# Long convolution of a Hyena layer: the inverse transform computed for half the rows with the table stationary, against the full transform with the spectrum stationary

## The chip, the core and the metric

The kernel runs on one core of a Trainium2 chip. The core has five engines with a queue each: TensorE (PE, matrix products into PSUM), VectorE (DVE), ScalarE (ACT), GpSimd (POOL) and SyncE (SP, which issues the DMAs here). The metric is the device time of one execution in microseconds.

## The reference, cut to what matters

Four layers work on 256 context tokens and 256 latent tokens, 1024 features each. Layer 2 (of 0 to 3) mixes tokens with a Hyena block, and this is the only place that the change touches:

```python
def fft_longconv(u, k):
    L = u.shape[1]
    U = jnp.fft.rfft(u.astype(F32), n=2 * L, axis=1)
    K = jnp.fft.rfft(k, n=2 * L, axis=0)
    return jnp.fft.irfft(U * K[None], n=2 * L, axis=1)[:, :L].astype(u.dtype)

def hyena(h, w_in, b_in, w_short, b_short, ..., skip, w_out, b_out):
    u = dwconv(h @ w_in + b_in, w_short, b_short)
    x0, x1, v = jnp.split(u, 3, axis=-1)
    k = hyena_filter(L, ...)          # divided by the sum of its absolute values
    v = v * x1
    v = fft_longconv(v, k) + skip * v
    return (v * x0) @ w_out + b_out
```

It is run for the context and for the latent stream, so L is 256 and each transform has 512 points.

## The kernel before

Everything is fp32. A weight or an operand `a` of a product is split into a rounded part and the rest (`hi` and `lo`, type fp32r), and `mm3` (L157 to L160) makes a product of three matmuls: hi by hi, hi by lo, lo by hi. `load_w` (L144, L147) makes the two parts of each weight tile: ACT copies the rounded part, DVE subtracts. `split` (L169, L170) does the same for activations, again one ACT and one DVE instruction.

The layer holds its features on partitions: `V[o]`, o from 0 to 7, is the product v * x1 of 128 features, with 512 columns: 256 context tokens (stream s = 0), then 256 latent tokens (s = 1). The transforms are matrix products with tables. A unit of the transform, m from 0 to 7, is one stream (s = m mod 2) of the 256 features of the tiles o = 2 (m div 2) and o + 1.

- On the way in, the sequence is folded about its middle: `PQ` holds sums and differences of token n and token 255 - n, for n below 128. `flip_in(m)` (L1261) transposes these with four PE transposes, so that tokens lie on partitions, and splits them.
- `freq(m, f)` makes the frequencies of half f (f = 0 or 1) with 6 matmuls of 256 columns, multiplies them by the filter's spectrum (L1275 to L1279 on DVE, one copy on POOL, L1281) and splits the result `Y[m, f]` (L169 on ACT, L170 on DVE).
- `back(m, c)` (L1285) makes the tokens of tile o = 2 (m div 2) + c: four `mm3`, 12 matmuls. `Y` is stationary (128 frequencies by 128 features) and the table `inv` moves with 256 columns, one for each token. So the result has features on partitions, as V has. DVE then multiplies V by `skip` in place (L1294) and adds the result scaled by `rn` (L166, `g<-mm,rn,g`).

`conv()` is a generator that lays these pieces out in 21 steps, st = 0 to 20. In step st come, in this order, `flip_in(m)` if it is due (st = 2m + 1 for even m, st = 2m for odd m), `freq(st div 2 - 1, st mod 2)` if there is one, and from st = 5 on `back((st - 5) div 2, (st - 5) mod 2)`. One step is taken behind every input projection (`in_proj`: 24 matmuls of 512 columns). Twelve steps stand beside the projections of v and x1, eight beside those of x0. The last step stands alone, behind step 19 and ahead of the output projection. Behind each projection `short` runs a 3-tap convolution: two ACT instructions (L1241, L1242) and two on DVE (L166, `e<-e,par`). In the steps of x0, `gate(o)` multiplies V by x0 (L1329) and splits it (L169, L170) for the output projection, whose loop takes the tiles k = 0 to 7 in order.

The order of PE's instructions is the order of the code. That of DVE, ACT and POOL is chosen by a scheduler ahead of the run, and each of these engines then takes its instructions strictly in that order, waiting in front of any whose input is missing.

Of the kernel before, what the change touches and what calls it, by code (L numbers as in the profile page):

```python
# [15 lines left out]
AF = mybir.ActivationFunctionType  # L16
ALU = mybir.AluOpType
AX = mybir.AxisListType

P = 128  # L20
D = 1024
KT = D // P
T = 512
L = 256
# [32 lines left out]
def r(ap):  # L57
    return ap.bitcast(F32R)
# [25 lines left out]
def kernel(ctx: ExitStack, tc: tile.TileContext, xT, cT, cB, ada0, ada2, adaT1, adaT2, adaT3, prm, mlp, w_c, w_ug, w_o,  # L84
                         w_p1, w_p2, w_hi1, w_hi0, w_ho, w_fup, w_fd0, w_fd1, w_fd2, spec0, f_w3, decay, dft, c_dft, c_b, out,
                         layers=(0, 1, 2, 3), final=True):
    nc = tc.nc
# [8 lines left out]
    def ps_mm():  # L96
        return pm.tile([P, T], F32, tag="mm", name="mm")

    def ps_tr():
        return pm.tile([P, T], F32, tag="mm", name="tr")  # L100
# [4 lines left out]
    def e_tile(shape=None):  # L105
        return gp.tile(shape or [P, T], F32, tag="g", name="e")

    ident = const.tile([P, P], F32, name="ident")
# [12 lines left out]
    def col(name, *dims):  # L121
        o, n = COLS[name]
        return par[:, o:o + n]
# [31 lines left out]
    def mm3(ps, a, b, start, stop):  # L155
        ah, al = a
        bh, bl = b  # L157
        nc.tensor.matmul(out=ps, lhsT=r(ah), rhs=r(bh), start=start, stop=False)  # L158
        nc.tensor.matmul(out=ps, lhsT=r(ah), rhs=r(bl), start=False, stop=False)  # L159
        nc.tensor.matmul(out=ps, lhsT=r(al), rhs=r(bh), start=False, stop=stop)  # L160

    def both(t, f):
        return f(t[0]), f(t[1])

    def stt(o, a, s, b, op0, op1, **kw):
        nc.vector.scalar_tensor_tensor(out=o, in0=a, scalar=s, in1=b, op0=op0, op1=op1, **kw)  # L166
# [945 lines left out]
    rn = const.tile([P, KT], F32, name="rn")  # L1112
# [102 lines left out]
    def hyena(li, nm):  # L1215
# [10 lines left out]
        inv = both(di, lambda t: t.rearrange("p (k t) -> p k t", k=4))  # L1226
# [26 lines left out]
        V, VT, Y, PQ = [], {}, {}, {}  # L1253
        skip = col("hy_skip")

        def flip_in(m):
            jj, s = divmod(m, 2)
            tr = ps_tr()
            for t in range(2):
                for c in range(2):  # L1260
                    nc.tensor.transpose(out=tr[:, (2 * t + c) * P:(2 * t + c + 1) * P], in_=PQ[2 * jj + c][:, t, s, :], identity=ident)  # L1261
            VT[m] = (g_tile(), g_tile())
            split(VT[m][0], VT[m][1], tr)

        def freq(m, f):
            jj, s = divmod(m, 2)
            vt = VT[m]
            ps = ps_mm()
            for im in range(2):
                fc = 2 * im + f  # L1270
                mm3(ps[:, im * L:(im + 1) * L], both(fwd, lambda a: a[:, fc * P:(fc + 1) * P]),
                    both(vt, lambda a: a[:, im * L:(im + 1) * L]), True, True)
            t1, t2 = e_tile(), e_tile()
            kk = kfs[jj // 2][:, jj % 2, f]
            nc.vector.tensor_tensor(out=two(t1), in0=two(ps), in1=kk, op=ALU.mult)  # L1275
            nc.vector.tensor_tensor(out=t2[:, 0:L], in0=ps[:, 0:L], in1=kk[:, 1], op=ALU.mult)
            nc.vector.tensor_tensor(out=t2[:, L:T], in0=ps[:, L:T], in1=kk[:, 0], op=ALU.mult)
            nc.vector.tensor_tensor(out=t2[:, L:T], in0=t2[:, 0:L], in1=t2[:, L:T], op=ALU.subtract)
            nc.vector.tensor_tensor(out=t2[:, 0:L], in0=t1[:, 0:L], in1=t1[:, L:T], op=ALU.add)  # L1279
            if f == 0:  # L1280
                nc.gpsimd.tensor_copy(out=t2[0:1, :], in_=t1[0:1, :])  # L1281
            Y[m, f] = (g_tile(), g_tile())
            split(Y[m, f][0], Y[m, f][1], t2)

        def back(m, c):  # L1285
            jj, s = divmod(m, 2)
            o = 2 * jj + c
            ps = ps_mm()
            for f in range(2):
                for im in range(2):  # L1290
                    mm3(ps[:, 0:L], both(Y[m, f], lambda a: a[:, im * L + c * P:im * L + (c + 1) * P]),
                        both(inv, lambda a: a[:, 2 * im + f, :]), f == 0 and im == 0, f == 1 and im == 1)
            vo = V[o][:, s * L:(s + 1) * L]
            nc.vector.tensor_scalar(out=vo, in0=vo, scalar1=skip[:, o:o + 1], scalar2=None, op0=ALU.mult)  # L1294
            stt(vo, ps[:, 0:L], rn[:, o:o + 1], vo, ALU.mult, ALU.add)

        def conv():
            for st in range(21):
                m, i = divmod(st, 2)
                if m < 8 and i == 1 - m % 2:  # L1300
                    flip_in(m)
                if 0 <= m - 1 < 8:
                    freq(m - 1, i)
                if st >= 5:
                    back((st - 5) // 2, (st - 5) % 2)
                yield

        work = conv()
        for o in range(KT):
            if o >= 2:  # L1310
# [24 lines left out]
        for u in range(4):  # L1335
            w = load_pair(w_hi0[u], act=True)
            for c in range(2):
                o = 2 * u + c
# [221 lines left out]
```

## Time and profile before

| | us |
|---|---|
| median of 3 runs (2144.52 to 2145.59) | 2145.06 |
| the profiled execution, its own time | 2145.16 |
| its span | 2143.3 |
| PE busy in the span | 2096.1 (98%) |
| DVE busy | 1557.3 (73%) |
| ACT busy | 1287.5 (60%) |
| POOL busy | 236.2 (11%) |

The time of the execution is 1.86 us above the span of its instructions. Matmuls overlap: a busy PE says that some matmul was in flight, and what a matmul costs is read from the distance between the starts of two. DVE and ACT instructions also overlap a little at their ends. A matmul named `mm<-a,b` streams `a` and holds `b`. The Hyena layer's transforms lie between 1240 us and 1377 us of the span. TensorE's granted clock there is 1.00, the upper of its two levels (2.4 GHz).

### The profile page before, as it was taken

How to read it: one execution, taken by the hardware profiler on the slowest of the kernel's cores; microseconds unless marked ns; L12 is line 12 of the kernel's file. 1: busy time of each engine (PE TensorE's matmuls, PEld its weight loads, DVE VectorE, ACT ScalarE, POOL GpSimd, SP SyncE). 2: the span in 40 equal slices, each digit the busy share in tenths (PEclk: the TensorE clock that was granted, in tenths of full speed). 3: DMA queues.
4: the chain of work that ended last, by engine and by line, in shares of the span. 5: the costliest groups of instructions: out<-in, count | busy, mean ns of one | idle time of the engine just before them, and what ended most of it. 6: DMA issues, size and time to landing. Idle time of an engine off the chain costs nothing.

```text
span 2143.3 us, 32063 instructions
## 1 busy us (share of the span) xinstructions
PE 2096.1 (98%) x12108; PEld 1801.3 (84%) x12108; DVE 1557.3 (73%) x2780; ACT 1287.5 (60%) x2774; POOL 236.2 (11%) x403
## 2 busy tenths in 40 slices
PE   7999999999999999999999999999999998899999
PEld 5767898888899979888888988898888888669999
DVE  5878368889756665768775689757979856976665
ACT  3788457778644465547654544456868745875453
POOL 0375200000020012000000200020000002621000
PEclk8999999999999999999999999999999999999999
DMA  8533135545432152444542322224545531114552
GB/s 316 211 131 139 60 118 179 214 177 200 173 128 84 59 205 81 155 150 163 196 171 85 114 85 93 99 79 158 210 182 196 197 113 50 58 46 171 180 189 85
DMA packets 48699, 305.39 MB, mean 142 GB/s; under 512 B 5536, under 2 KB 6688, under 8 KB 16160
## 3 DMA queue, kind: packets, MB, share of 16 engines
q1 hardware_dynamic: 47824, 300.91, 39.8%
q8 instruction: 95, 1.56, 0.3%
q10 hardware_dynamic: 720, 2.44, 0.3%
q14 instruction: 60, 0.49, 0.1%
HBM read 299.13 MB, written 4.19 MB: 142 GB/s over the span
## 4 chain that ended last, share of the span: by engine, by line
PE 89%; DVE 4%; ACT 3%; POOL 2%; DMA 1%; issue 1%; SPq 0%; POOLq 0%; ACTq 0%; DVEq 0%
PE mm L158 26%; PE mm L159 25%; PE mm L160 25%; PE mm L463 4%; PE mm L469 2%; PE mm L850 1%; PE ada L243 1%; PE tr L829 1%; PE mm L636 1%; ACT g L761 1%; DMA x<-in_xT_dram 1%; PE tr L357 1%; PE idle L221 1%; POOL e L337 1%; PE mm L642 0%
## 5 line engine op out<-in xcount | busy, mean ns | idle before, releaser
L158 PE MATMUL mm<-hh,whi 128*128 128x512 f32 (+1 forms) x1856 | 657.2, 354 | 0.0
L159 PE MATMUL mm<-hl,whi 128*128 128x512 f32 (+1 forms) x1856 | 654.5, 353 | 0.0
L160 PE MATMUL mm<-hh,wlo 128*128 128x512 f32 (+1 forms) x1856 | 654.2, 352 | 0.0
L147 DVE TENSOR_TENSOR wlo<-raw,whi 128x1024 fp32r<-128x1024 f32 (+2 forms) x361 | 430.0, 1193 | 290.4 <-PE mm L159 179.2
L144 ACT ACTIVATE whi<-raw 128x1024 fp32r<-128x1024 f32 (+3 forms) x370 | 374.6, 1017 | 293.9 <-PE mm L160 160.7
L158 PEld LDWEIGHTS mm<-hh,whi 128*128 128x128 f32 x1856 | 351.1, 189 | 51.7 <-issue 3.1
L160 PEld LDWEIGHTS mm<-hh,wlo 128*128 128x128 f32 x1856 | 351.0, 189 | 47.7
L159 PEld LDWEIGHTS mm<-hl,whi 128*128 128x128 f32 x1856 | 351.2, 189 | 46.3
L285 ACT ACTIVATE e<-e 128x512 f32<-128x512 f32 x512 | 315.9, 619 | 80.8 <-DVE e L284 80.5
L284 DVE TENSOR_TENSOR e<-raw,e 128x512 f32<-128x512 f32 x512 | 315.3, 684 | 0.0
L158 PE MATMUL mm<-g,whi 128*128 128x512 f32 (+1 forms) x904 | 309.1, 342 | 0.0
L159 PE MATMUL mm<-g,whi 128*128 128x512 f32 (+1 forms) x904 | 307.5, 340 | 0.0
L160 PE MATMUL mm<-g,wlo 128*128 128x512 f32 (+1 forms) x872 | 298.5, 342 | 0.0
L337 POOL TENSOR_TENSOR e<-e 128x256 f32<-128x256 f32 (+1 forms) x63 | 70.2, 1114 | 1209.7 <-ACT e L335 1176.6
L158 PEld LDWEIGHTS mm<-g,whi 128*128 128x128 f32 x904 | 171.3, 189 | 19.7
L159 PEld LDWEIGHTS mm<-g,whi 128*128 128x128 f32 x904 | 171.3, 190 | 19.6
L160 PEld LDWEIGHTS mm<-g,wlo 128*128 128x128 f32 x872 | 165.3, 190 | 19.0
L169 ACT ACTIVATE g<-e 128x512 fp32r<-128x512 f32 (+1 forms) x137 | 76.3, 558 | 106.4 <-DVE e L534 45.3
L166 DVE SCALAR_TENSOR_TENSOR e<-mm,par,e 128x510 f32<-128x510 f32 (+3 forms) x186 | 126.2, 678 | 15.6 <-ACT e L528 11.6
L166 DVE SCALAR_TENSOR_TENSOR x<-mm,mod,x 128x256 f32<-128x256 f32 x192 | 85.3, 477 | 52.0 <-PE mm L160 51.8
L170 DVE TENSOR_TENSOR g<-e,g 128x512 fp32r<-128x512 f32 (+1 forms) x137 | 81.9, 598 | 41.8 <-ACT g L169 41.4
L528 ACT ACTIVATE e<-mm,par 128x512 f32<-128x512 f32 (+1 forms) x88 | 63.0, 716 | 63.7 <-PE mm L160 59.2
(264 smaller groups left out, 2856.1 us busy)
## 6 DMA issues: line engine op xcount, KB each, us to landing
raw<-in_w_fup_dram SPq DMA_DIRECT2D x88, 1024.0 KB, 4.9
raw<-in_adaT_dram SPq DMA_DIRECT2D x64, 1024.0 KB, 4.8
raw<-in_w_fd_dram SPq DMA_DIRECT2D x32, 1024.0 KB, 4.9
raw<-in_ada_dram SPq DMA_DIRECT2D x29, 1024.0 KB, 5.2
raw<-in_w_fd_dram SPq DMA_DIRECT2D x16, 768.0 KB, 4.2
raw<-in_w_p_dram SPq DMA_DIRECT2D x12, 1024.0 KB, 4.9
raw<-in_w_hi_dram SPq DMA_DIRECT2D x12, 1024.0 KB, 5.0
raw<-in_w_o_dram SPq DMA_DIRECT2D x8, 1024.0 KB, 4.9
```

The costliest lines, as they stand in the source:

```text
L144: nc.scalar.activation(out=r(hi[:, 0:n]), in_=part, func=AF.Copy)
L147: nc.vector.tensor_tensor(out=r(lo[:, 0:n]), in0=part, in1=hi[:, 0:n], op=ALU.subtract)
L158: nc.tensor.matmul(out=ps, lhsT=r(ah), rhs=r(bh), start=start, stop=False)
L159: nc.tensor.matmul(out=ps, lhsT=r(ah), rhs=r(bl), start=False, stop=False)
L160: nc.tensor.matmul(out=ps, lhsT=r(al), rhs=r(bh), start=False, stop=stop)
L166: nc.vector.scalar_tensor_tensor(out=o, in0=a, scalar=s, in1=b, op0=op0, op1=op1, **kw)
L169: nc.scalar.activation(out=r(hi), in_=src, func=AF.Copy)
L170: nc.vector.tensor_tensor(out=r(lo), in0=src, in1=hi, op=ALU.subtract)
L284: nc.vector.tensor_tensor(out=t, in0=raw[:, q * D + (i % 2) * T:q * D + (i % 2 + 1) * T], in1=sb[i], op=ALU.mult)
L285: nc.scalar.activation(out=t, in_=t, func=AF.Copy, accum_out=asum[:, 2 * u + q, i // 2, i % 2:i % 2 + 1])
L337: self.eng.tensor_tensor(out=self.acc[:, a:b], in0=self.acc[:, a:b], in1=t[:, a:b], op=ALU.add)
L463: nc.tensor.matmul(out=banks[i][q][:, v], lhsT=r(wq[:, k, :]), rhs=r(HH[:, k, v]), start=k == 0 and wq is w[i][q][0], stop=False)
```

## The change

`back` is no longer called per tile of features but once for a unit m, in the odd steps, and `flip_out` takes the even ones. `back(m)` uses the symmetry of the table about the middle of the sequence: the cosine rows give a part that is even about it, the sine rows one that is odd. For tokens 0 to 127 it makes both, each as two `mm3` with the table stationary (`inv[..., 0:P]`, 128 frequencies by 128 tokens) and `Y` moving with 256 features: 12 matmuls, tokens on partitions. ACT copies the odd part out of PSUM, and DVE forms the sum (tokens 0 to 127) and the difference (tokens 255 down to 128) in `sd`. One step later `flip_out(m)` transposes the four 128 by 128 blocks of `sd` on PE, and DVE scales them and adds them to V with four instructions of 128 columns, two of which write backwards. The product with `skip` moves from DVE to POOL.

```diff
-        def back(m, c):
+        SD = {}
+
+        def back(m):
+            ps, sd = ps_mm(), e_tile()
+            for im in range(2):
+                for f in range(2):
+                    mm3(ps[:, im * L:(im + 1) * L], both(inv, lambda a: a[:, 2 * im + f, 0:P]),
+                        both(Y[m, f], lambda a: a[:, im * L:(im + 1) * L]), f == 0, f == 1)
+            odd = e_tile()[:, 0:L]
+            nc.scalar.activation(out=odd, in_=ps[:, L:T], func=AF.Copy)
+            for d, op in enumerate((ALU.add, ALU.subtract)):
+                nc.vector.tensor_tensor(out=sd[:, d * L:(d + 1) * L], in0=ps[:, 0:L], in1=odd, op=op)
+            SD[m] = sd
             jj, s = divmod(m, 2)
-            o = 2 * jj + c
-            ps = ps_mm()
-            for f in range(2):
-                for im in range(2):
-                    mm3(ps[:, 0:L], both(Y[m, f], lambda a: a[:, im * L + c * P:im * L + (c + 1) * P]),
-                        both(inv, lambda a: a[:, 2 * im + f, :]), f == 0 and im == 0, f == 1 and im == 1)
-            vo = V[o][:, s * L:(s + 1) * L]
-            nc.vector.tensor_scalar(out=vo, in0=vo, scalar1=skip[:, o:o + 1], scalar2=None, op0=ALU.mult)
-            stt(vo, ps[:, 0:L], rn[:, o:o + 1], vo, ALU.mult, ALU.add)
+            for o in (2 * jj, 2 * jj + 1):
+                vo = V[o][:, s * L:(s + 1) * L]
+                nc.gpsimd.tensor_scalar(out=vo, in0=vo, scalar1=skip[:, o:o + 1], scalar2=None, op0=ALU.mult)
+
+        def flip_out(m):
+            jj, s = divmod(m, 2)
+            sd, tr = SD.pop(m), ps_tr()
+            for c in range(2):
+                for d in range(2):
+                    nc.tensor.transpose(out=tr[:, (2 * c + d) * P:(2 * c + d + 1) * P], in_=sd[:, d * L + c * P:d * L + (c + 1) * P],
+                                        identity=ident)
+            for c in range(2):
+                o = 2 * jj + c
+                vo = V[o][:, s * L:(s + 1) * L]
+                for d, v in enumerate((vo[:, 0:P], vo[:, L - 1:P - 1:-1])):
+                    stt(v, tr[:, (2 * c + d) * P:(2 * c + d + 1) * P], rn[:, o:o + 1], v, ALU.mult, ALU.add)
...
                 if st >= 5:
-                    back((st - 5) // 2, (st - 5) % 2)
+                    (back, flip_out)[(st - 5) % 2]((st - 5) // 2)
```

In the changed kernel the odd copy is L1294 on ACT, the sum and difference L1296 on DVE, the product with `skip` L1301 on POOL and the new transposes L1308.

On PE an even step loses its 12 matmuls and gets four transposes; the odd steps keep 12 matmuls with operands exchanged. The last rows of the first even step with a way back (st = 6), where `mm<-g,whi` above is `freq` and `mm<-hh,whi` below the next projection:

```order
 L160 MATMUL mm<-g,whi 128x256
-L158 MATMUL mm<-whi,g 128x256
-L159 MATMUL mm<-wlo,g 128x256
-L160 MATMUL mm<-whi,g 128x256
-L158 MATMUL mm<-whi,g 128x256
-L159 MATMUL mm<-wlo,g 128x256
-L160 MATMUL mm<-whi,g 128x256
-L158 MATMUL mm<-whi,g 128x256
```
```order
+L1308 MATMUL tr<-ident,e 128x128 x4
 L158 MATMUL mm<-hh,whi 128x512
 L159 MATMUL mm<-hl,whi 128x512
```

Twelve rows go (the first seven are shown), and one group of four comes.

On DVE, around the first way back (unit 0). In the kernel before `mm_12360` is the result of `back(0, 0)`, made in step 5, `mm_12449` that of `back(0, 1)` in step 6, and `g_12357` is the lo part of `Y[1, 1]`:

```order
L166 SCALAR_TENSOR_TENSOR g_12021<-mm_12360,rn_102,g_12021 128x256
L170 TENSOR_TENSOR g_12299<-e_12291,g_12298 128x512
L166 SCALAR_TENSOR_TENSOR e_12328<-e_12327,par_87,e_12328 128x2x255
L170 TENSOR_TENSOR g_12339<-tr_12333,g_12338 128x512
L166 SCALAR_TENSOR_TENSOR e_12328<-e_12327,par_87,e_12328 128x2x255
```
```order
L147 TENSOR_TENSOR wlo_12689<-raw_12686,whi_12688 128x1024
L170 TENSOR_TENSOR g_12357<-e_12350,g_12356 128x512
L1319 TENSOR_TENSOR g_12375<-e_12328,e_12278 128x512
L166 SCALAR_TENSOR_TENSOR g_12038<-mm_12449,rn_102,g_12038 128x256
```

The same place now; `e_12361` is `sd` of unit 0, made from `mm_12360` (step 5), and `tr_12454` is the result of `flip_out(0)` in step 6:

```order
L147 TENSOR_TENSOR wlo_12692<-raw_12689,whi_12691 128x1024
L170 TENSOR_TENSOR g_12357<-e_12350,g_12356 128x512
L1296 TENSOR_TENSOR e_12361<-mm_12360,e_12374 128x256 x2
L1338 TENSOR_TENSOR g_12380<-e_12328,e_12278 128x512
L166 SCALAR_TENSOR_TENSOR g_12021<-tr_12454,rn_102,g_12021 128x128
```

What DVE did with `mm_12360` stood ahead of the split of `Y[1, 0]` (`g_12299`); now it stands behind the split of `Y[1, 1]`, and the transposes wait for it.

On ACT, at the end of the stage (`mm_13360` and `mm_13353` are the last projection of x0 before and now, `mm_13384` the result of `back(7)`, `e_13398` the odd part; L169 is the split of the last two gated tiles). Before:

```order
L1241 ACTIVATE e_13385<-mm_13360,par_87 128x512
L1242 ACTIVATE e_13386<-mm_13360,mid_12006,par_87 128x512
L144 ACTIVATE whi_13580<-raw_13578 128x1024
L169 ACTIVATE g_13422<-g_12681 128x512
L144 ACTIVATE whi_13584<-raw_13578 128x1024
```

Now:

```order
L1241 ACTIVATE e_13378<-mm_13353,par_87 128x512
L1242 ACTIVATE e_13379<-mm_13353,mid_12006,par_87 128x512
L144 ACTIVATE whi_13572<-raw_13570 128x1024
L1294 ACTIVATE e_13398<-mm_13384 128x256
L144 ACTIVATE whi_13576<-raw_13570 128x1024
```

The odd copy stands behind a weight tile's rounding, and the sum, the difference and the last four transposes come behind it.

## Rows read from the trace of the kernel before

**Rows 1.** The page: busy time by engine, and the chain that ended last.

```profile
PE 2096.1 (98%) x12108; PEld 1801.3 (84%) x12108; DVE 1557.3 (73%) x2780; ACT 1287.5 (60%) x2774; POOL 236.2 (11%) x403
...
PE 89%; DVE 4%; ACT 3%; POOL 2%; DMA 1%; issue 1%; SPq 0%; POOLq 0%; ACTq 0%; DVEq 0%
```

**Rows 2.** Windows: stretch, then PE, PEld, DVE, ACT, POOL busy, clock, DMA.

```profile
1275.90:1353.82 77.92, 77.92 (x438) 68.15 (x437) 70.31 (x133) 32.90 (x50) 3.38 (x5) 1.00 0.24 82
```

**Rows 3.** Timeline of PE, step 16: start, duration, engine, line, operation.

```profile
1351.67 0.28 PE L158 MATMUL mm<-g,whi 128*128 128x256 f32 x1
...
1352.38 0.28 PE L158 MATMUL mm<-whi,g 128*128 128x256 f32 x1
...
1353.82 0.40 PE L158 MATMUL mm<-hh,whi 128*128 128x512 f32 x1
```

**Rows 4.** Timeline of PE, `flip_in(0)` and what follows it.

```profile
1240.34 0.60 PE L1261 MATMUL tr<-ident,e 128*128 128x128 f32 x4
1240.70 0.48 PE L158 MATMUL mm<-hh,whi 128*128 128x512 f32 x1
1241.01 0.40 PE L159 MATMUL mm<-hl,whi 128*128 128x512 f32 x1
1241.25 0.40 PE L160 MATMUL mm<-hh,wlo 128*128 128x512 f32 x1
```

**Rows 5.** DVE groups by shape, 1275.90 to 1353.82: count, busy, mean ns, idle before.

```profile
L166 DVE SCALAR_TENSOR_TENSOR e<-e,par 128x510 f32<-128x510 f32 x20 | 14.8, 740 | 0.0
L147 DVE TENSOR_TENSOR wlo<-raw,whi 128x1024 fp32r<-128x1024 f32 x11 | 13.5, 1226 | 4.6 <-ACT whi L144 4.6
L170 DVE TENSOR_TENSOR g<-e,g 128x512 fp32r<-128x512 f32 x10 | 6.9, 687 | 2.8 <-ACT g L169 2.8
...
L166 DVE SCALAR_TENSOR_TENSOR g<-mm,rn,g 128x256 f32<-128x256 f32 x10 | 4.8, 477 | 0.0
...
L1294 DVE TENSOR_SCALAR g<-g,par 128x256 f32<-128x256 f32 x8 | 3.0, 390 | 0.0
```

**Rows 6.** Groups by shape of the whole span, DVE, ACT and POOL.

```profile
L734 DVE TENSOR_REDUCE hst<-e 128x4 f32<-128x128 f32 x24 | 6.6, 275 | 0.0
...
L1195 ACT ACTIVATE e<-mm 128x256 f32<-128x256 f32 x16 | 5.1, 384 | 1.6 <-PE mm L160 1.6
...
L817 POOL TENSOR_SCALAR g<-g,sm 128x256 f32<-128x256 f32 x32 | 30.6, 969 | 28.0 <-DVE sm L814 26.1 <-PE mm L160 1.9
```

**Rows 7.** Timeline of step 6: PE, ACT and DVE around `back(0, 1)`.

```profile
1274.46 0.28 PE L158 MATMUL mm<-whi,g 128*128 128x256 f32 x1
...
1274.85 0.63 ACT L169 ACTIVATE g<-e 128x512 fp32r<-128x512 f32 x1 [0.46 <-DVE e L1279]
...
1275.86 0.69 DVE L170 TENSOR_TENSOR g<-e,g 128x512 fp32r<-128x512 f32 x1
...
1276.46 0.68 DVE L1319 TENSOR_TENSOR g<-e 128x512 f32<-128x512 f32 x1
```

**Rows 8.** Timeline of DVE: a split directly behind the spectrum product.

```profile
1318.83 0.41 DVE L1279 TENSOR_TENSOR e<-e 128x256 f32<-128x256 f32 x1
1319.94 0.69 DVE L170 TENSOR_TENSOR g<-e,g 128x512 fp32r<-128x512 f32 x1 [0.70 <-ACT g L169]
```

**Rows 9.** Timeline of the last two steps: PE, ACT and DVE.

```profile
1373.81 0.28 PE L158 MATMUL mm<-whi,g 128*128 128x256 f32 x1
...
1375.32 1.05 ACT L144 ACTIVATE whi<-raw 128x1024 fp32r<-128x1024 f32 x1
...
1375.46 0.75 DVE L166 SCALAR_TENSOR_TENSOR e<-e,par 128x510 f32<-128x510 f32 x1 [0.45 <-ACT e L1242]
1376.13 0.48 DVE L166 SCALAR_TENSOR_TENSOR g<-mm,rn,g 128x256 f32<-128x256 f32 x1
```

**Rows 10.** Timelines of POOL and DVE behind the stage.

```profile
1392.57 1.28 POOL L337 TENSOR_TENSOR e<-e 128x512 f32<-128x512 f32 x1 [32.34 <-DMA raw<-in_w_fup_dram]
...
1393.00 1.93 DVE L147 TENSOR_TENSOR wlo<-raw,whi 128x1024 fp32r<-128x1024 f32 x1 [1.24 <-PE mm L159]
```

## The prediction, made before the changed kernel ran

> **What bounds the kernel now.** I read the busy times by engine and the chain of waits first: PE works 98% of the span and holds 89% of the chain that ended last [rows 1]. So the kernel's time is PE's time, and a microsecond taken from PE counts if nothing makes PE wait in its place. Next I read the windows of the stage that the change touches. Between 1275.90 and 1353.82 us (steps 7 to 16) PE is busy for the whole 77.92 us at a granted clock of 1.00, the upper level. The reader is to see the number two columns on: DVE is busy for 70.31 us of these 77.92 [rows 2]. DVE is no bound there, but it has only 7.6 us to spare, 0.76 us in each of ten steps. The DVE groups of the same window say what the rest is: 4.6 us of waiting for the rounding of weights on ACT, and 2.8 us for the hi part of the split on ACT [rows 5]. The first kind is paced by PE, which frees the weight tiles, and vanishes when DVE is late. The second does not: the spectrum product ends, ACT makes the hi part, DVE waits 0.70 us for it [rows 8].
>
> **PE's share of the change.** In step 16 the 6 matmuls of `freq` start at 1351.67, the 12 of `back` at 1352.38, the next projection at 1353.82: 12 matmuls cost 1.44 us on PE, 0.12 us each [rows 3]. Eight even steps lose them: 8 x 1.44 = 11.5 us. In the odd steps `back` keeps 12 matmuls of 256 columns, with one weight load each as before, so I cost the exchange of operands at nothing. Each even step gets four transposes of the kind that `flip_in` has: 0.36 us from the first to the next matmul, and 0.31 in place of 0.24 us for that one, so 0.43 us [rows 4]. Eight of them are 3.4 us. PE's own work falls by 11.5 - 3.4 = 8.1 us, 1.01 in each even step.
>
> A transpose by the Trainium skill (TensorE: Matmul & The Clock Gate, Part 4: PE-mode transpose) takes about 275 ns in a kernel's midst. By that figure four would be 1.1 us, and PE's work would fall by only 8 x 0.34 = 2.7 us. The rows have four in 0.43 us, since they follow one another in the pipeline, and I go by them.
>
> **What PE now has to wait for.** Before, nothing on PE waited for the way back soon: DVE took the result from PSUM when it came to it. Now `flip_out(m)` waits for the sum and difference (L1296), which wait for ACT's odd copy (L1294), and for whatever stands ahead of these in DVE's and ACT's queues. Behind the waiting transposes stands the next projection, and everything else of PE. Three places:
>
> *The first, step 6.* `back(0)` ends in step 5, but its odd copy and its sum stand behind the split of `Y[1, 1]`, which comes in step 6. Until then nothing differs on this path, so the times of before hold. PE would begin `flip_out(0)` where `back(0, 1)` began, at 1274.46. ACT is at that split at 1274.85 and would make the odd copy (0.38 us, L1195 [rows 6]) by 1275.9; DVE starts its half of the split at 1275.86 and its next instruction at 1276.46 [rows 7]. From there the sum takes 0.33 and the difference 0.41 us (a sum of 256 columns: 0.41, with an overlap of 0.08 [rows 8]): 1277.2. PE waits 1277.2 - 1274.5 = 2.8 us.
>
> *The middle, steps 7 to 16.* Here I make a budget of DVE. Instructions overlap by 0.08 us at their ends (L170 of 0.69 us, the next after 0.60 [rows 7]). Out go 8 products with skip (0.34 - 0.08 = 0.26; two of the eight are longer [rows 5]), 2.1 us, and 10 scaled sums of 256 columns (0.477 - 0.08 = 0.40), 4.0 us. In come 10 sums or differences of 256 columns (0.33), 3.3 us, and 20 scaled sums of 128 columns. No row has those. From 510 columns in 0.740 and 256 in 0.477 us [rows 5] a line gives 0.345 us, 0.27 with the overlap, so 5.4 us; a reduction of 128 columns at 0.275 us [rows 6] bounds them from below at 0.20, the 0.40 of 256 columns from above: 4.0 to 8.0 us. I take the line's value, as its rows are of the same operation. DVE then has 70.3 - 2.1 - 4.0 + 3.3 + 5.4 = 72.9 us of work. PE's ten steps shrink by 5 x 1.01 to 72.9 us. The two are equal, and DVE's work is no longer a stretch that PE can outlast: sum and difference of each unit stand close ahead of DVE's wait for the same unit's transposes, so neither engine can run more than about 1 us ahead of the other. Whatever DVE waits for is then PE's loss. In the new order five of the ten splits stand directly behind their spectrum product with nothing between (those of f = 1, units 2 to 6): 5 x 0.70 = 3.5 us [rows 8], and the others I put at 0.8 us together, as a weight tile's subtraction covers most of their round trip over POOL and ACT. DVE needs 72.9 + 4.3 = 77.2 us, so PE waits 4.3 us here. Bounds: none at all, if DVE's work is at the low end and its waits are covered; and 10 us, if the 7.6 us of idle time stay as they are and the 128-column sums cost 0.40.
>
> In steps 18 and 19 there is no `freq` left, DVE has its five products less to make, and I charge nothing.
>
> *The end, steps 19 and 20.* Between `back(7)` and `flip_out(7)` stands no projection. Let `back` begin at 0 (1373.81 before); it ends at 1.44. ACT has the last projection's two instructions and the rounding of a weight tile first, which starts at 1375.32 - 1373.81 = 1.51 and lasts 1.05, then the odd copy until about 2.9. DVE starts the projection's first tap at 1.65 and has 0.67 us from start to start, so it is free after the second at 2.99 [rows 9]. Sum and difference end at 3.73. PE waits 3.73 - 1.44 = 2.3 us. The output projection's tiles 6 and 7 then come 3 to 4 us later than before; six tiles of 1.4 us (6 matmuls of 0.24 each [rows 4]) stand ahead of them, so that costs nothing.
>
> The odd copies add 8 x 0.38 = 3.1 us to an ACT that is busy for 32.9 of 77.9 us [rows 2, 6]; they are priced only where they stand in the path above. The 16 products on POOL (0.97 us each [rows 6]) stand a step or more ahead of their use. No DMA is added or moved.
>
> **The sum.** -8.1 + 2.8 + 4.3 + 2.3 = +1.3 us, against the profiled execution's 2145.16 us, which lies 0.1 above the median of the three runs: 2146.5 us. Behind the stage PE bounds again, so the difference is handed on as it is. With the bounds of the middle, 0 and 10, the sum runs from -3.0 to +7.0: 2142.2 to 2152.2 us. This is my forecast: the work saved on PE is paid back in waits, because DVE has no room.
>
> **The rivals.**
>
> *PE's saving arrives.* If DVE takes sum and difference early, PE waits only at the end, where nothing stands between: -8.1 + 2.3 = -5.8, 2139.4 us. For it: PE is the bound everywhere now, and DVE has never made it wait in this stage. Against it: the order of DVE's and ACT's queues at step 6, which is fixed. Half of this, with the first wait but none in the middle, is the lower bound above, 2142.2 us.
>
> *POOL holds up DVE.* The products with skip run on POOL beside DVE. In the rows a subtraction on DVE that usually takes 1.23 us took 1.93 when it started at 1393.00, while POOL worked from 1392.57 to 1393.85: it ended 1.08 us behind POOL's end, about as if it had begun there [rows 5, 10]. Eight products fall into the middle steps, when V of tiles 4 to 7 is made. If each holds DVE for its whole 0.97 us [rows 6], a DVE without room passes on 7.8 us: 2146.5 + 7.8 = 2154.3 us. It decides the sign, that is it goes beyond what a measurement can tell from no change, from about 0.37 us of each product on (3.0 us more, 4.3 in all). Against it: in the new order a product comes just behind the folding of its tile, where DVE has mostly sums with one operand in PSUM, and only the operation of two SBUF operands shows the wait in the rows.
>
> The Trainium skill says the same as a rule (SBUF — State Buffer, SBUF: two separate sides): GpSimd and a VectorE operation with two SBUF inputs take a common port in turn, each for a whole instruction. The rows above agree in the one case; by the rule every such meeting would be lost time, and the time would be up to 2154.3 us.
>
> **How the numbers follow.** The forecast has a chance of 0.52; the lower bound without waits in the middle 0.18; the saving that arrives 0.10; POOL or a dearer DVE 0.20. A difference of 0.2%, 4.3 us, is about what a measurement tells from no change. Faster than 2140.8: the third case and a little of the second, 0.12. Slower than 2149.4: the fourth and the forecast's upper end, 0.27. The rest, 0.61, is within 0.2%. The range runs from 2141.0 to 2151.5; it leaves out most of the arriving saving and the far half of POOL's case.
>
> **What would show it.** In the changed kernel's profile PE should be idle for some 9 us of the stage, put down to the transposes L1308 waiting for DVE's L1296. `flip_out(0)` should start near 1277.3, the last one some 2.3 us behind the last matmul of `back(7)`. DVE should be busy for over 93% of steps 7 to 16. Wrong: L1308 waits for nothing except at the end (then the saving arrives), or DVE's two-operand instructions are stretched whenever L1301 runs (then POOL does it).

## The result, and the profile after

The changed kernel takes 2163.86 us (median of 4 runs, 2160.41 to 2164.11), the kernel before 2144.79 us beside it: ratio 1.0084, 95% interval 1.0068 to 1.0100. Four more runs gave 2162.51 us and 1.0077 (1.0062 to 1.0092). So it is 17 to 19 us slower; the prediction said 2146.5 and a range up to 2151.5. The profiled execution took 2164.11 us, 18.95 more than that of before.

The page's busy times and chain, which answer to [rows 1]:

```profile
PE 2104.3 (97%) x12044; PEld 1803.1 (83%) x12044; DVE 1560.9 (72%) x2796; ACT 1289.9 (60%) x2782; POOL 254.0 (12%) x419
...
PE 88%; DVE 4%; ACT 4%; POOL 2%; issue 1%; DMA 1%; SPq 0%; ACTq 0%; POOLq 0%; DVEq 0%
```

PE has 64 instructions fewer and is busy 8 us longer. Something made the same matmuls slower. Next the waits between 1230 and 1420 us: who waited for whom, us in total, times, longest.

```profile
PE tr L1308 <- DVE e L1296: 13.0, 6, 3.2
```

All of PE's waiting is at the new place: the transposes of `flip_out` wait for sum and difference. The first one on PE's timeline, at `flip_out(0)`:

```profile
1277.77 0.28 PE L160 MATMUL mm<-g,whi 128*128 128x256 f32 x1
1280.37 1.17 PE L1308 MATMUL tr<-ident,e 128*128 128x128 f32 x4 [2.32 <-DVE e L1296]
1281.19 0.78 PE L158 MATMUL mm<-hh,whi 128*128 128x512 f32 x1
1281.76 0.63 PE L159 MATMUL mm<-hl,whi 128*128 128x512 f32 x1
1282.19 0.63 PE L160 MATMUL mm<-hh,wlo 128*128 128x512 f32 x1
```

Three things are to be seen. PE could have begun 0.12 us behind the last 256-column matmul, at 1277.89, and began at 1280.37: a wait of 2.48 us. The four transposes then take 0.82 us to the next matmul, where `flip_in`'s took 0.36 [rows 4]. And the matmuls behind them start 0.43 us apart, where 512 columns took 0.23 to 0.24 [rows 4]. The windows show TensorE's clock there (stretch, its length, then PE, PEld, DVE, ACT and POOL busy, PE's granted clock, DMA):

```profile
1281.19:1366.79 85.60, 78.91 (x398) 66.65 (x397) 73.53 (x146) 34.21 (x53) 11.40 (x13) 0.94 0.22 74
1280.37:1284.29 3.92, 3.92 (x11) 3.09 (x12) 3.59 (x10) 0.54 (x2) 1.44 (x2) 0.56 0.00 0
1348.00:1352.00 4.00, 4.00 (x11) 3.12 (x10) 4.00 (x11) 0.00 (x0) 0.00 (x0) 0.50 0.00 0
750.00:800.00 50.00, 47.22 (x340) 35.39 (x339) 30.26 (x91) 30.03 (x69) 4.83 (x5) 0.93 0.52 187
1243.78:1431.61 187.83, 174.86 (x905) 149.00 (x904) 140.37 (x260) 77.89 (x119) 23.85 (x27) 0.95 0.23 79
```

Behind four of the six waits, at `flip_out(0)`, `(4)`, `(5)` and `(7)`, the granted clock is at its lower level (1.2 GHz, a clock of 0.50) for some 3 us, and behind `flip_out(4)` for some 6 us. The fourth row is another stage, 450 us ahead of the change, where the clock fell too. The last row is the whole stage, from `flip_in(0)` to the first matmul of L357, which follows in the output projection; before, the same work took 172.52 us at a clock of 1.00:

```profile
1240.34:1412.86 172.52, 172.52 (x969) 151.13 (x968) 135.95 (x241) 75.38 (x111) 11.27 (x14) 1.00 0.25 86
```

So the stage is 15.31 us longer, 3.4 us were lost ahead of it (`flip_in(0)` starts at 1243.78 in place of 1240.34), and 0.2 lies behind it.

Why does the sum come late? ACT and then DVE ahead of `flip_out(4)`, the longest wait (PE was free at 1343.03 and got its sum at 1346.39):

```profile
1341.90 1.06 ACT L144 ACTIVATE whi<-raw 128x1024 fp32r<-128x1024 f32 x1 [4.22 <-issue]
1344.64 0.63 ACT L169 ACTIVATE g<-e 128x512 fp32r<-128x512 f32 x1 [1.69 <-DVE e L1279]
1345.18 0.37 ACT L1294 ACTIVATE e<-mm 128x256 f32<-128x256 f32 x1
```

```profile
1342.99 1.23 DVE L147 TENSOR_TENSOR wlo<-raw,whi 128x1024 fp32r<-128x1024 f32 x1 [1.03 <-ACT whi L144]
1344.13 0.42 DVE L1279 TENSOR_TENSOR e<-e 128x256 f32<-128x256 f32 x1
1345.31 0.69 DVE L170 TENSOR_TENSOR g<-e,g 128x512 fp32r<-128x512 f32 x1 [0.76 <-ACT g L169]
1345.91 0.75 DVE L1296 TENSOR_TENSOR e<-mm,e 128x256 f32<-128x256 f32 x2
```

One chain from engine to engine: the projection ends (its last matmul starts at 1341.65) and ACT rounds the next weight (1341.90), DVE waits 1.03 us for it, subtracts, ends the spectrum product, waits 0.76 us for its hi part, splits, and only then makes the sum. `back(4)` had ended long before; its odd copy (L1294) stood on ACT behind the hi part, its sum on DVE behind all of it. PE has only `flip_in` and one `freq` between the end of the projection and the transposes. For this rounding the profile names no releaser ("issue"); for the six others in steps 7 to 16 that waited it is PE:

```profile
ACT whi L144 <- PE mm L159: 21.4, 6, 7.5
```

DVE's groups in steps 7 to 16, which answer to [rows 5] (busy, mean ns, then idle time before them):

```profile
L147 DVE TENSOR_TENSOR wlo<-raw,whi 128x1024 fp32r<-128x1024 f32 x10 | 12.5, 1253 | 7.3 <-ACT whi L144 7.3
...
L170 DVE TENSOR_TENSOR g<-e,g 128x512 fp32r<-128x512 f32 x10 | 6.9, 687 | 3.6 <-ACT g L169 3.6
L166 DVE SCALAR_TENSOR_TENSOR g<-tr,rn,g 128x128 f32<-128x128 f32 x20 | 6.2, 345 | 0.9 <-PE tr L1308 0.7
```

DVE's wait for rounded weights did not vanish. It rose from 4.6 to 7.3 us, and the section on the prediction shows how much of that the low clock added. The last wait, which answers to [rows 9], is PE's at `flip_out(7)`:

```profile
1390.93 0.28 PE L160 MATMUL mm<-g,wlo 128*128 128x256 f32 x1
1393.13 1.23 PE L1308 MATMUL tr<-ident,e 128*128 128x128 f32 x4 [1.93 <-DVE e L1296]
```

### The profile page after: what moved, and what is told of

Read it like the earlier page. It is cut to its first block, busy times and chain, and to the rows that moved or that the text cites. A ratio compares the mean times of both kernels' runs of the same rounds, so it can differ in the third digit from the quotient of the medians.

```text
span 2162.3 us, 31984 instructions
## 1 busy us (share of the span) xinstructions
PE 2104.3 (97%) x12044; PEld 1803.1 (83%) x12044; DVE 1560.9 (72%) x2796; ACT 1289.9 (60%) x2782; POOL 254.0 (12%) x419
## 4 chain that ended last, share of the span: by engine, by line
PE 88%; DVE 4%; ACT 4%; POOL 2%; issue 1%; DMA 1%; SPq 0%; ACTq 0%; POOLq 0%; DVEq 0%
PE mm L158 25%; PE mm L159 25%; PE mm L160 25%; PE mm L463 4%; PE mm L469 2%; PE mm L850 1%; PE ada L243 1%; PE tr L829 1%; PE mm L636 1%; ACT g L761 1%; DMA x<-in_xT_dram 1%; PE tr L357 1%; DVE wlo L147 1%; PE idle L221 1%; POOL e L337 1%
## 5 line engine op out<-in xcount | busy, mean ns | idle before, releaser
L158 PE MATMUL mm<-g,whi 128*128 128x512 f32 (+1 forms) x936 | 318.9, 341 | 0.0
L159 PE MATMUL mm<-g,whi 128*128 128x512 f32 (+1 forms) x936 | 317.0, 339 | 0.0
L160 PE MATMUL mm<-g,wlo 128*128 128x512 f32 (+1 forms) x904 | 308.0, 341 | 0.0
L158 PEld LDWEIGHTS mm<-g,whi 128*128 128x128 f32 x936 | 177.9, 190 | 19.7
L159 PEld LDWEIGHTS mm<-g,whi 128*128 128x128 f32 x936 | 177.9, 190 | 19.6
L160 PEld LDWEIGHTS mm<-g,wlo 128*128 128x128 f32 x904 | 171.7, 190 | 19.2
L169 ACT ACTIVATE g<-e 128x512 fp32r<-128x512 f32 (+1 forms) x137 | 76.3, 558 | 125.9 <-DVE e L534 46.1
L166 DVE SCALAR_TENSOR_TENSOR e<-mm,par,e 128x510 f32<-128x510 f32 (+3 forms) x186 | 126.2, 678 | 14.6 <-ACT e L528 10.7
L170 DVE TENSOR_TENSOR g<-e,g 128x512 fp32r<-128x512 f32 (+1 forms) x137 | 81.9, 598 | 44.2 <-ACT g L169 43.8
```

Source lines behind the costliest of these rows:

```text
L169: nc.scalar.activation(out=r(hi), in_=src, func=AF.Copy)
L170: nc.vector.tensor_tensor(out=r(lo), in0=src, in1=hi, op=ALU.subtract)
```

## The experiments

Two theories to begin with. *Order*: sum and difference stand too close ahead of their transposes, and a step's distance ends the waits. *Throughput*: DVE has too much work, and a wait that is removed comes back elsewhere. Beside them: that products on GpSimd hold DVE up, and that the low clock is a price of its own. Each result is a median with its runs' range, and the ratio to the kernel before with its 95% interval.

One limit holds for most of them. The scheduler orders the queues of DVE, ACT and POOL anew for each kernel. With the skip product on DVE and with dummy matmuls the order on DVE and ACT is that of the changed kernel (the products put in); in the other runs it differs in more than the edit, so what they gain or lose belongs to edit and new order together.

**One step later.**

```
-if st >= 5:
-    (back, flip_out)[(st - 5) % 2]((st - 5) // 2)
+if st >= 5 and st % 2:
+    if st < 20: back((st - 5) // 2)
+    if st >= 7: flip_out((st - 7) // 2)
...
```

Left out here: `conv()` has one step more, and the gates of tiles 4 and 5 both come behind the sixth projection of x0.

> flip_out(m) moved one step later, behind back(m+1), so that a whole step of PE work lies between back(m) and its transposes; everything else as in the changed kernel. Order theory (the sum and difference stand too close ahead of the transposes, PE waits about 14 us, and each wait lets the granted clock fall): the waits at flip_out(0) to (6) and the clock's falls behind them go, the wait at the end stays (about 2 us, with 1.5 us of clock behind it); 2145 - 8.1 + 2 + 1.5 = about 2140 us, 2143.5 if the fall of the clock near 770 us comes again. Throughput theory (DVE has no room: 77 us needed in a stretch where PE has 73): the waits only move, about 10 us of them remain, about 2150 us or more.

2154.59 us (2153.69 to 2155.36), 1.0040 (1.0025 to 1.0055). Its waits:

```profile
PE tr L1308 <- DVE e L1296: 5.2, 2, 4.7
PE tr L1261 <- DVE e L1346: 4.1, 1, 4.1
PE mm L159 <- DVE g L170: 2.3, 2, 1.3
PE mm L158 <- ACT g L169: 0.4, 1, 0.4
```

The waits at `flip_out(0)` to `(6)` are gone, as order has it, and 12.0 us of others have come: `flip_in(6)` for its tile's folding (L1346), matmuls for a split (L170), the last transposes. The clock fell behind two of them (0.96 over the stage). The place of the sum alone is not the cause.

**The skip product on DVE.** The edit: `nc.gpsimd.tensor_scalar` of L1301 becomes `nc.vector.tensor_scalar`.

> The skip product is back on DVE (L1301), everything else as in the changed kernel. POOL theory (products on POOL hold DVE up): the time falls by some us, to about 2155-2158. Order theory: 16 products of 0.34 us more on DVE, most of them ahead of the next unit's work; the waits of the transposes become longer rather than shorter, 2164 to 2170 us.

2162.07 us (2155.25 to 2165.09), 1.0070 (1.0048 to 1.0092). The profiled run is the one of 2155.25:

```profile
PE tr L1308 <- DVE e L1296: 13.0, 6, 3.2
```

```profile
1239.63:1422.11 182.48, 169.49 (x906) 144.53 (x905) 144.21 (x273) 78.03 (x119) 10.93 (x14) 0.99 0.23 81
```

The waits are the same to the digit, so GpSimd is not what makes PE wait. That they would grow with more work on DVE did not come either: in steps 7 to 16 DVE works for 75.66 in place of 73.53 us, and waits 2.3 in place of 7.3 us for rounded weights. What differs for PE is the clock: it fell behind one wait only, that at `flip_out(6)`, 0.99 over the stage. With equal waits its stage is 5.4 us shorter than the changed kernel's (182.48 and 187.83), and its own other runs go up to 2165.

**PE busy during the wait.** Dummy matmuls ahead of the transposes (in the table `FILL` their number by unit).

```
+if FILL[m]:              # FILL = (9, 0, 5, 0, 13, 8, 8, 7)
+    warm_up(FILL[m])
 sd, tr = SD.pop(m), ps_tr()
```

> As the changed kernel, with dummy matmuls on PE ahead of the transposes of flip_out(0), (2), (4), (5), (6), (7), about as long as the wait there, so that PE is busy while DVE makes sum and difference. If the granted clock falls because PE is idle in the waits, it stays at the upper level here: the time falls by what the low clock cost, 8 to 10 us, to about 2155 us (2152 if the fall near 770 us is not there either), with the waits themselves kept. If the clock's falls have another cause, the time stays at 2164 us or rises.

2153.12 us (2152.47 to 2157.43), 1.0037 (1.0025 to 1.0049).

```profile
1239.51:1420.05 180.54, 178.48 (x1006) 154.61 (x1004) 140.46 (x260) 78.14 (x119) 24.02 (x27) 1.00 0.24 82
```

The transposes start as late as before (2.1 us of recorded waits are left, the rest is dummies), the clock stays at 1.00, and the time falls by 9 to 11 us, 3.4 of them the fall near 770 us where it was there. The clock's fall belongs to PE's idle time and is a price of its own.

**Transposes of a tile that is ready.** The edit: `in_=sd[...]` of L1308 becomes the same slice of `x[:, 0]`.

> As the changed kernel, but the transposes of flip_out read a tile that has long been ready in place of sum and difference (so the output leaves out the convolution's result); DVE, ACT and POOL have the same instructions. PE then waits for nothing there. If PE's own saving is 8.1 us as worked out and DVE has room for its work, the time is 2145 - 8.1 = 2137 us (2140 with the fall near 770 us). If DVE or POOL are too slow by themselves, PE waits elsewhere, for PSUM or for the split, and the time stays above 2145 us.

2147.94 us (2147.11 to 2152.44), 1.0016 (1.0006 to 1.0025). Its waits:

```profile
PE tr L1261 <- DVE e L1343: 3.8, 1, 3.8
PE mm L159 <- DVE g L170: 1.8, 3, 1.0
PE mm L158 <- ACT g L169: 1.5, 3, 0.8
```

PE waits for nothing in `flip_out`, and still loses 7.1 us to DVE and to ACT's hi parts. Nothing ties the transposes to the sum now, and the scheduler has put DVE's and ACT's queues in quite another order: in steps 7 to 16 DVE works for 68.9 and waits for 10.7 of 80.0 us, 7.2 of them for hi parts. So DVE's work and its waits for ACT hold PE up without `flip_out` too, which is throughput as a cause; how much is work and how much this order, the run does not tell apart.

**The changed kernel again.**

> The changed kernel itself once more. If the fall of the clock near 770 us (3.4 us, in code that the change does not touch) and the falls behind the waits are a matter of chance, its runs spread between about 2153 us (no fall) and 2164 us (all falls), as those with the skip product on DVE did (2155 to 2165). If they belong to this kernel, all runs lie near 2160 or 2164 us again.

2159.67, 2160.74, 2164.27, 2164.92 us. In the profiled one (2160.74) the waits are the same 13.0 us, the clock over the stage 0.95 again, and near 770 us nothing fell:

```profile
750.00:800.00 50.00, 47.22 (x366) 37.24 (x365) 31.82 (x93) 31.81 (x72) 5.30 (x6) 1.00 0.57 211
```

So the 3.4 us lost there come and go from run to run. The falls in the stage stand behind the same four waits as in the first profile: they belong to this kernel. Two kernels below show that fall in their profiles too (0.93), with the same code there.

**Later, with less work on DVE.** On the delayed kernel:

```
+mirror = const.tile([P, P], F32, name="mirror")
+nc.vector.tensor_copy(out=mirror, in_=ident[:, ::-1])
...
-identity=ident)
+identity=mirror if d else ident)
...
-for d, v in enumerate((vo[:, 0:P], vo[:, L - 1:P - 1:-1])):
-    stt(v, tr[:, (2*c+d)*P:(2*c+d+1)*P], rn[:, o:o+1], v, ...)
+stt(vo, tr[:, c*L:(c+1)*L], rn[:, o:o+1], vo, ...)
...
-tensor_tensor(out=t2[:, 0:L], in0=ps[:, 0:L], in1=kk[:, 1], ...)
-tensor_tensor(out=t2[:, L:T], in0=ps[:, L:T], in1=kk[:, 0], ...)
+tensor_tensor(out=two(t2), in0=two(ps), in1=kk[:, ::-1], ...)
```

> The kernel with flip_out one step later (2154.6 us), with less work on DVE: the transposes of the differences go against a mirrored identity, so that the two scaled sums of 128 columns (0.345 us each) become one of 256 (0.477), and the two products of 256 columns with kf become one of 512. By rows about 0.13 us less for each of 16 sums and 0.07 for each of 16 products, 3 us over the stage. Throughput theory (DVE's work and its waits for ACT set the pace): 2151 to 2152 us, and less if a fall of the clock goes too. Order theory: no gain, 2154 us.

2146.66 us (2146.30 to 2150.12), 1.0010 (1.0001 to 1.0020).

```profile
PE tr L1309 <- DVE e L1297: 5.5, 2, 4.9
PE mm L161 <- DVE g L172: 1.0, 1, 1.0
PE mm L160 <- ACT g L171: 0.4, 1, 0.4
```

8 us for 3 us of DVE's work, more than either theory expected: the wait for the folding and the fall of the clock behind it are gone, the wait and the fall at the end are left.

**The same without the delay.**

> The changed kernel with the mirrored identity and the merged product (about 3 us less work on DVE over the stage), flip_out where the change has it. If it is the place of sum and difference in DVE's queue that makes the transposes wait, the six waits stay nearly as they are, 12 to 14 us, and the time is 2153 to 2162 us, as the clock falls. If DVE's amount of work alone does it, the waits ahead of the end (11.8 us) shrink by the 3 us or more, and with the falls of the clock the time comes down to about 2150 us.

2153.81 us (2148.68 to 2156.41), 1.0031 (1.0020 to 1.0043).

```profile
PE tr L1309 <- DVE e L1297: 7.9, 5, 2.0
```

13.0 us of waits became 7.9: neither remedy is enough alone. Relief without delay leaves 7.9 us of waits, delay without relief 12.0, both 6.9, most of it at the end.

**Sums on GpSimd**, with delay and relief:

```
-nc.scalar.activation(out=odd, in_=ps[:, L:T], func=AF.Copy)
+nc.scalar.activation(out=eo, in_=ps, func=AF.Copy)
...
-    nc.vector.tensor_tensor(out=sd[...], in0=ps[:, 0:L], in1=odd, op=op)
+    nc.gpsimd.tensor_tensor(out=sd[...], in0=eo[:, 0:L], in1=eo[:, L:T], op=op)
```

> The kernel before it in this list, with sum and difference on GpSimd (about 1 us each) from a copy that ACT makes of both parts: DVE loses 16 instructions of 0.335 us net, 5.4 us more over the stage, and the way from back to the transposes no longer passes DVE's queue. Throughput theory: 2145 to 2147 us, without most of the falls of the clock down to 2143. If products on GpSimd hold DVE up, DVE's instructions of two SBUF operands are stretched and the time is 2150 us or more.

2142.90 us (2141.77 to 2146.42), 0.9990 (0.9980 to 0.9999).

```profile
PE tr L1309 <- POOL e L1297: 2.6, 2, 1.8
PE tr L1263 <- DVE e L1346: 0.4, 1, 0.4
```

GpSimd does hold DVE up: in steps 7 to 16 DVE is busy for 67.9 us, 67.4 in the kernel before it in this list, though ten instructions of 0.335 us have left it. So the gain is not a freer DVE. The last wait is 1.8 in place of 4.9 us, and the waits for a split are gone.

**The last part inside the output projection.** The end of the stage moves into the first unit of `proj_out`:

```
+def last():
+    for _ in work: pass
+    gate(6); gate(7)
...
+            if late is not None and k == 2:   # in tail, u == 0; late = last
+                late()
```

> The kernel before it in this list, with the last flip_out and the last two gates issued inside the first unit of the output projection, behind its third k tile, so that PE has work while the last sum is made. The wait at the end (2 to 3 us, and the low clock behind it) goes: 2 to 5 us less than the kernel before it. If the two last gates come too late for the k tiles 6 and 7, a wait appears there in its place and the time stays.

2138.53 us (2138.23 to 2139.91), 0.9964 (0.9952 to 0.9977): this version beats both kernels.

```profile
PE tr L1265 <- DVE e L1348: 0.4, 1, 0.4
```

```profile
1241.26:1407.04 165.78, 165.32 (x905) 142.99 (x904) 136.88 (x212) 79.40 (x119) 45.93 (x43) 1.00 0.26 89
1283.35:1357.02 73.67, 73.23 (x399) 63.13 (x398) 67.89 (x110) 35.27 (x53) 22.58 (x21) 1.00 0.25 86
```

```profile
L149 DVE TENSOR_TENSOR wlo<-raw,whi 128x1024 fp32r<-128x1024 f32 x10 | 12.8, 1283 | 0.3 <-ACT whi L146 0.3
```

PE is busy all through, the clock stays up, and DVE hardly waits for rounded weights any more: 0.3 us in steps 7 to 16, where the changed kernel had 7.3 (for hi parts it still waits 4.9). The second row is those steps.

**That version without the delay.**

> The version that beat both kernels (2138.5 us: mirrored identity, merged product, sums on GpSimd, last part inside the output projection), but with flip_out where the change has it, not one step later. If the delay is what keeps PE from waiting, waits of 1 to 3 us come back at the transposes: 2142 to 2150 us. If it is enough that the sums are out of DVE's queue, the time stays at 2138 to 2139 us.

2158.44 us (2155.55 to 2160.88), 1.0057 (1.0042 to 1.0072).

```profile
PE tr L1311 <- POOL e L1299: 13.3, 12, 2.5
```

The delay is worth 20 us here, with the slower sums of GpSimd, far more than I expected. That the sums leave DVE's queue is not enough.

**Sums on GpSimd alone**, in the changed kernel:

> The changed kernel with sum and difference on GpSimd, from a copy that ACT makes of both parts, and nothing else. Way from back to the transposes: copy 0.7 us, two instructions of about 1 us on GpSimd, so 2.8 us, while PE has a projection of 5.6 us in between; DVE's queue is no longer on the way. If the queue is the cause, the waits at flip_out(0) to (6) go, and only the end has one, of about 3 us: 2145 - 8.1 + 3 + 1.5 of low clock = about 2141.5 us, and up to 2146 if DVE still falls behind elsewhere. If GpSimd's instructions wait behind its others (two skip products of 1 us, a row copy) or hold DVE up, waits stay and the time is above 2150 us.

2170.43 us (2168.61 to 2176.14), 1.0118 (1.0100 to 1.0135); 24 us above the most that I expected if DVE's queue were the cause. At `flip_out(0)`, on ACT, GpSimd and PE (PE was free at 1273.77):

```profile
1274.16 0.63 ACT L169 ACTIVATE g<-e 128x512 fp32r<-128x512 f32 x1 [0.46 <-DVE e L1279]
1274.69 0.58 ACT L1294 ACTIVATE e<-mm 128x512 f32<-128x512 f32 x1
...
1275.35 2.22 POOL L1296 TENSOR_TENSOR e<-e 128x256 f32<-128x256 f32 x2 [7.37 <-ACT e L1294]
...
1276.49 0.33 PE L1308 MATMUL tr<-ident,e 128*128 128x128 f32 x1 [2.57 <-POOL e L1296]
1277.63 0.55 PE L1308 MATMUL tr<-ident,e 128*128 128x128 f32 x3 [0.81 <-POOL e L1296]
```

ACT's copy stands behind the hi part of the split, which waits for DVE. The late queue is ACT's as much as DVE's, and GpSimd takes 1.1 us for each sum where DVE takes 0.33.

**The best version with the sums on DVE.**

> The version of 2138.5 us with sum and difference on DVE, as the change has them (delay, mirrored identity, merged product and the last part inside the output projection stay). By rows DVE has 5.4 us more work over the stage, and of the kernel without the last part's move (2146.7 us) the waits at its end, 4.9 us and the low clock behind them, go: about 2140 to 2141 us. If DVE's queue is late there all the same, the wait moves to the k tiles 6 and 7 of the output projection: 2143 us or more.

2142.14 us (2140.16 to 2145.38), 0.9985 (0.9975 to 0.9994). The profiled run (2144.19) has the fall near 770 us; PE's waits in the stage are 2.9 us. The median lies between my two cases. With a step of distance the sums on GpSimd are worth 2 to 4 us: 3.6 by the medians, 1.9 from the fastest run to the fastest.

## Why the prediction was wrong

It was made of terms that can be set against the profiled execution, 18.95 us in all.

*PE's own work, -8.1 us: right.* In the best version, where almost nothing waits, steps 7 to 16 have PE busy for 73.23 us; the prediction said 72.9. The stage is 6.74 us shorter there, with 0.9 us of waits left (at `flip_in(6)` and the last transposes); 0.5 us stays open.

*The first wait, 2.8 us: right,* 2.48. *The end, 2.3 us: right,* 2.08.

*The middle, 4.3 us: too small.* DVE's work was right (72.9 said, 73.53 in the window), and so was the picture of a DVE without room: it works or waits for 85.1 of the window's 85.60 us. Its waits were not right. The step that failed is the sentence that the waits for rounded weights are "paced by PE, which frees the weight tiles, and vanishes when DVE is late". PE frees a tile at the end of a projection however late DVE is; and in the new order PE waits for DVE, so that each wait puts off the next freeing. What the term measures shows where the clock stays up: DVE's waits in steps 7 to 16 (81.31 us) of the run with dummy matmuls, where all lines are one further down.

```profile
DVE wlo L148 <- ACT whi L145: 3.6, 6, 1.1
DVE g L171 <- ACT g L170: 3.6, 5, 0.8
```

For rounded weights it is 3.6 us where I put nothing, for hi parts 3.6 where I put 4.3: DVE needs 73.6 + 3.6 + 3.6 = 80.8 us, and 77.2 were forecast. The 7.3 us of the changed kernel hold what the low clock adds: a slower PE frees its tiles later. DVE is busy for 90% of these steps here and for 86% in the changed kernel; over 93% had been forecast.

The sum stood behind that weight on DVE, and the whole chain of 4.4 us fell into the time of one `freq`. PE lost 1.53, 3.36 and 2.28 us at `flip_out(2)`, `(4)`, `(5)`: 7.2. At `(6)`, in step 18, where I charged nothing, it lost 2.18, and there the loop stands in one row of DVE:

```profile
1381.22 1.23 DVE L147 TENSOR_TENSOR wlo<-raw,whi 128x1024 fp32r<-128x1024 f32 x1 [0.80 <-PE mm L159]
```

DVE waits until PE's projection ends (its last matmul starts at 1381.02), then subtracts, splits and makes the sum from 1382.96 on; PE waits for it until 1383.43. All six waits together: 13.9 us where 9.4 were forecast.

*The transposes, 0.43 us for four: right only if the tile is ready.* Where the sum has only just been made they take 0.57 to 0.64 us to the next matmul at the upper clock, and not 0.36, since the second one waits for the difference, which DVE makes 0.33 us behind the sum: about 0.27 more, at seven of the eight, 1.8 us. In the best version all but one group keep the distances of [rows 4], and so it was right to go by the rows. The 275 ns for one that the Trainium skill gives (TensorE: Matmul & The Clock Gate, Part 4: PE-mode transpose) agree with the length of a single transpose here, 0.27 us; from start to start it is 0.11 us, and that is the price in a row.

*The clock: missing from the sum.* This is the second step that failed, and the largest part of the miss. I read a clock of 1.00 in the windows of before and took it over for a kernel in which PE would wait. From one `flip_out` to the next, set against the profiled run with the skip product on DVE, which has the same waits: 1.5 us behind `(0)`, 2.7 behind `(4)`, 1.5 behind `(5)`, 1.6 behind `(7)`, together 7.3 us. The run with dummy matmuls shows the same from the other side: with the waits kept and the clock at 1.00 its profiled run took 2152.83 us, and 2145.16 - 8.1 + 13.9 + 1.8 is 2152.8.

*Near 770 us:* 3.4 us of low clock in code that the change does not touch, in some runs and not in others. The kernel before also has runs some 3 us above its others (about one in five, up to 2149.25 us); none of these was profiled. Whether the change makes the fall there more frequent stays open.

The sum is -8.1 + 13.9 + 1.8 + 7.3 + 3.4 = 18.3 of 18.95 us. With right waits and no clock term the prediction would have been 2152.8, still outside its range.

*The rivals.* "PE's saving arrives" fell, though it is what the best version reaches, with a step of distance, less work on DVE and the end of the stage moved. "POOL holds up DVE" fell for the changed kernel with the second experiment: without the products on GpSimd the waits are the same. But the effect is real, and the best version shows it, where GpSimd makes the sums too:

```profile
1307.56 2.43 POOL L1299 TENSOR_TENSOR e<-e 128x256 f32<-128x256 f32 x2 [8.39 <-ACT e L1297]
1308.17 1.23 DVE L1343 TENSOR_TENSOR g<-e 128x512 f32<-128x512 f32 x1
```

DVE's product takes 0.69 us where it meets no instruction of GpSimd. Here it ends at 1309.40, 0.6 us behind the end of GpSimd's first sum (about 1308.8), as if it had begun there. In this stage such products take 1.09 in place of 0.69 us on the mean where they meet one, foldings 0.87 in place of 0.42, weights' subtractions 1.43 in place of 1.22; products with an operand in PSUM keep their 0.68. Together I estimate some 8 us of DVE's time in the stage from these means, 0.5 us in steps 7 to 16 of the changed kernel, where the prediction's rival had up to 7.8. The rule that the prediction cited from the Trainium skill (SBUF — State Buffer, SBUF: two separate sides), a common port taken in turn, each for a whole instruction, agrees with these rows. The best version pays it on DVE, and PE waits for DVE only 0.4 us there.

My order theory after the result was half of the truth, as delay and relief apart and together showed.

## What to carry to other kernels

Where an engine that sets the time is made to wait for one that did not hold it up before, look what stands ahead in that engine's queue and in the queues it waits for, and put a whole stage of work between; an instruction that hangs on something the waiting engine itself releases closes a loop. Count an idle TensorE twice, once for the wait and once for the clock that may fall behind it (here behind waits of 2 us and more, not behind each). And relieve the second engine in the same step: delay and relief gave 9 and 10 us apart, 17 together, and the version with all parts 25.

## What the runs showed of the hardware that was not expected

The granted clock fell to its lower level behind waits of 2.1 to 3.4 us in the changed kernel, not behind that of 1.53 us, and in the same run not behind one of 2.18. With the same six waits it fell behind one only in the profiled run with the skip product on DVE, and there behind that of 2.18. What decides between two equal waits stays open. Between 750 and 800 us, where PE is idle for 2.8 us in all, the clock falls in some executions (0.93) and not in others (1.00), in the same code.

A transpose against an identity with its columns mirrored reverses the columns of what it writes and takes as long as a plain one (0.11 us from start to start in the best version). It saved DVE an instruction for each pair.
